# A hybrid attention and RWKV-7 layer on one core: key norms and values by transposes with sums on VectorE, and a new order of the planned region

## The chip, the cores and the metric

The kernel runs on one core of a Trainium2 chip. The metric is the device time of one execution in microseconds (us). The engines are TensorE (PE, with its weight loads as PEld), VectorE (DVE), ScalarE (ACT), GpSimd (POOL) and SyncE (SP, which here issues most transfers). Each works through its own queue in order and waits on semaphores for the others. SBUF is the on-chip memory; PSUM is the accumulator memory that TensorE writes, eight buffers of 128 x 512 floats here.

## The reference

One decoder layer over 16 meta tokens and 512 tokens of width 1024, all in float32. A layer norm feeds one wide projection (w_in), whose columns serve sliding-window attention (16 query heads, 2 key/value heads, window 128, a sink per head, relative bias), an RWKV-7 time mix with 16 heads of 64, and two gates. The two branches are merged by sigmoid gates, projected (w_out), normed, passed through a squared-ReLU MLP of width 4096, and normed again. What the change touches is in the time mix:

```python
kk = kh * k_k
kk = kk / jnp.maximum(jnp.sqrt(jnp.sum(kk * kk, -1, keepdims=True)), 1e-12)   # key norms, per head and token
def step(S, inp):                                   # S: 64 x 64 per head
    sa = jnp.einsum('bhij,bhj->bhi', S, -kk_t)
    S = S * w_t[..., None, :] + sa[..., None] * (kk_t * a_t)[..., None, :] + v_t[..., None] * k_t[..., None, :]
    return S, jnp.einsum('bhij,bhj->bhi', S, r_t)
ym = jnp.mean(y, -1, keepdims=True)                 # per head and token
yv = jnp.mean(jnp.square(y - ym), -1, keepdims=True)
y = ((y - ym) * lax.rsqrt(yv + GN_EPS)) * lnx_g + lnx_b
```

## The kernel before

**Stages.** After the first layer norm (function `lead`), the activations lie transposed in SBUF as hhi and hlo, a high and a low part in the reduced format float32r. A weight block of 128 columns comes by DMA as wraw, is split by ACT (whi, L611) and DVE (wlo, L613), and three float32r products per slice (`three`, L454 to L456) add up to float32 precision. `dense` runs one such block; `shifted` adds the token shift at the eviction (ACT L653, DVE L656). Work that is not of this kind, the attention scores and the whole time mix, uses plain fp32 products or transposes against the constant ident.

**The time mix.** The 16 heads go in eight pairs, j = 0 to 7, each on 128 partitions (64 per head). `rwkv(j)` issues, for one pair: the projections k, r, v; sq, the squared scaled keys; `norms` (L984), which sums sq over the 64 rows of a head for each token by products with the constant ones2; from it d1, its maximum with 1e-24 and its reciprocal (L992, L994), spread by POOL into dv and dvx (L999, L1008). Eight chunks of 64 tokens then get score products (L1031), whose lower triangle NT is inverted: blocks go by DMA to DRAM and back as Nf, POOL does a substitution of 31 steps (L1122, L1126), the blocks come back by DMA as XB, and DVE transposes parts into U (L1153). Two small products (`inv3` L1146, `inv4` L1151) join the blocks. `fold_w` (L1166) and `fold_g` (L1182) fold the inverse into G, whose last additions are DVE L1186. `turn_v` (L1093) brings the values v to token order, and with the constant center (identity minus the mean over a head) removes the mean over the head's 64 values, so that the outputs come out with a mean of zero. `meta0` (L1193) does it for the meta tokens, whose own small chain is L1205, L1209, L1213. The chain over the chunks is seven `link` products (L1243), each followed by `follow`, which writes the new state Z (DVE L1225 for one head, ACT L1228 for the other). `outs` (L1253) gives Y in PSUM. Then the group norm: squares on ACT (L1264), their sum on DVE (L1265), scale and epsilon (L1266), the power -0.5 on POOL (L1267), the multiplication (L1268), and `turn_y` (L1273). The last pair does this in two halves of 256 columns, since nothing comes after it but the w_out products (`project_out`, L1418 to L1420) and the first norm of `first_norm` (L1482 to L1514).

**What sets the order.** All of this, from `lead` to the first up-projections, is a list of operations in a plan. Each operation names its engine, what it reads and writes, and a cost; each buffer belongs to a ring of a few tiles (rg is the ring of the eight PSUM buffers, named g in the trace). The table ORDER gives the sequence in which all operations are issued, hence the order on every engine, and SLOTS says which tile of its ring each buffer takes. The costs given to `op` are not used when the kernel is built. Behind the region comes the feed-forward part, which has an order written by due times of its own.

## Time and profile before

| what | value |
|---|---|
| median of 3 runs | 897.04 us (896.89 to 897.99) |
| profiled execution | 897.01 us, span 895.2 us, granted TensorE clock 0.994 |
| busy, TensorE / VectorE / ScalarE / GpSimd | 874.7 / 674.4 / 518.8 / 263.2 us |
| HBM traffic | 107.56 MB read, 8.21 MB written |

The span runs from the first to the last instruction on the core. Rows of the timeline read: start in us, duration in us, engine, line, operation, out<-in by the program's names, partitions and size, and the number of instructions that the row holds; in brackets the time that the engine was idle before it, and what ended that. A row of windows reads: stretch, its length, then busy time and number of instructions of TensorE, its weight loads, VectorE, ScalarE and GpSimd, the granted clock of TensorE, the busy share of the DMA engines and GB/s. Rows of one line's instructions give minimum, median and maximum in ns. Matmuls are pipelined, so a row's duration overlaps the next; the time that a product costs is the distance between starts.

### The profile page before, as it was taken

The numbers are of one execution on the slowest core, as the hardware profiler recorded it, in microseconds if no ns is written. First come the engines' busy times: TensorE is split into PE (matmuls) and PEld (weight loads), VectorE is DVE, ScalarE is ACT, GpSimd is POOL, SyncE is SP. The second block draws the span as 40 slices with busy tenths as digits, with TensorE's granted clock in tenths as the row PEclk, the third lists the DMA queues.
The fourth block names the chain that finished last, engine by engine and source line by source line (L and its number), as shares of the span: only waits on it lengthen the run. The fifth ranks groups of instructions, "written<-read, shape, count | busy, mean of one in ns | idle before, by whom it ended". The sixth has DMA issues, their size and how long they took to land.

```text
span 895.2 us, 17524 instructions
## 1 busy us (share of the span) xinstructions
PE 874.7 (98%) x6712; PEld 768.1 (86%) x6712; DVE 674.4 (75%) x1192; ACT 518.8 (58%) x1131; POOL 263.2 (29%) x672
## 2 busy tenths in 40 slices
PE   7999999999999999999989999999999999999996
PEld 6999989888898998887878877988898989888885
DVE  6882976868868678478497689598877896788757
ACT  7854568466575494483663745765556655564710
POOL 3138164183461721822816502000010000000001
PEclk9999999999999999999989999999999999999999
DMA  7443323424143242223243631395687578576322
GB/s 272 127 130 104 86 75 107 117 64 131 55 123 101 78 109 85 84 70 101 72 109 102 197 102 59 97 299 132 178 209 216 141 202 256 133 209 165 98 91 94
DMA packets 73533, 115.87 MB, mean 129 GB/s; under 512 B 40311, under 2 KB 47737, under 8 KB 69481
## 3 DMA queue, kind: packets, MB, share of 16 engines
q1 hardware_dynamic: 69728, 98.89, 35.5%
q0 software_dynamic: 2880, 14.68, 9.0%
q8 instruction: 53, 0.87, 0.4%
q10 hardware_dynamic: 840, 1.17, 0.4%
q14 instruction: 32, 0.25, 0.1%
HBM read 107.56 MB, written 8.21 MB: 129 GB/s over the span
## 4 chain that ended last, share of the span: by engine, by line
PE 90%; DVE 8%; issue 1%; ACT 1%; DMA 1%; POOL 0%; DVEq 0%; SPq 0%; ACTq 0%
PE g L454 12%; PE g L455 11%; PE g L456 11%; PE dnR L1798 7%; PE rq L1704 5%; PE tp L1704 4%; PE dnP L1798 4%; PE last L1798 4%; PE dnT L1798 3%; PE up L454 3%; PE up L455 3%; PE up L456 3%; PE g L1243 2%; PE g L1182 2%; PE g L1297 2%; PE g L1031 1%
## 5 line engine op out<-in xcount | busy, mean ns | idle before, releaser
L454 PE MATMUL g<-hhi,whi 128*128 128x512 f32 (+3 forms) x640 | 213.1, 333 | 0.2 <-DVE GR L1045 0.2
L455 PE MATMUL g<-hlo,whi 128*128 128x512 f32 (+3 forms) x640 | 204.0, 319 | 1.6 <-DVE hlo L817 1.6
L456 PE MATMUL g<-hhi,wlo 128*128 128x512 f32 (+3 forms) x640 | 203.6, 318 | 0.0
L454 PEld LDWEIGHTS g<-hhi,whi 128*128 128x128 f32 x640 | 121.0, 189 | 12.6 <-issue 2.2
L455 PEld LDWEIGHTS g<-hlo,whi 128*128 128x128 f32 x640 | 121.2, 189 | 9.6 <-DVE hlo L817 2.1
L456 PEld LDWEIGHTS g<-hhi,wlo 128*128 128x128 f32 x640 | 120.9, 189 | 8.5 <-DVE wlo L613 0.2
L613 DVE TENSOR_TENSOR wlo<-wraw,whi 128x512 fp32r<-128x512 f32 x126 | 88.3, 708 | 30.4 <-ACT whi L611 29.9
L1122 POOL TENSOR_TENSOR ftmp<-Xf,Nf 108x84 f32<-108x84 f32 (+23 forms) x248 | 86.8, 350 | 74.9 <-DMA Nf<-Nd 45.9
L611 ACT CAST whi<-wraw 128x512 fp32r<-128x512 f32 x126 | 77.0, 619 | 54.0 <-PE g L455 24.6
L1126 POOL TENSOR_TENSOR Xf<-Xf,ftmp 108x84 f32<-108x84 f32 (+23 forms) x248 | 89.6, 361 | 19.0
L1788 POOL DMA_DIRECT2D braw<-in_w_ff_dram x12 | 10.7, 890 | 206.1 <-DVE wlo L1605 87.2
L1228 ACT ACTIVATE Z<-g,PC 64x64 f32<-64x64 f32 x64 | 19.7, 308 | 65.2 <-DVE Z L1225 39.9
L1267 POOL TENSOR_TENSOR rs<-rs,mhalf 128x8 f32<-128x8 f32 (+1 forms) x9 | 14.9, 1659 | 76.2 <-DVE rs L1266 76.2
L1605 DVE TENSOR_TENSOR wlo<-wraw,whi 128x1024 fp32r<-128x1024 f32 x22 | 26.9, 1222 | 13.2 <-ACT whi L1601 10.6
L1225 DVE TENSOR_SCALAR Z<-g,PC 64x64 f32<-64x64 f32 x64 | 17.6, 274 | 23.3 <-PE g L1243 20.8
L1601 ACT CAST whi<-wraw 128x1024 fp32r<-128x1024 f32 x22 | 22.9, 1042 | 17.5 <-PE dnR L1798 8.7
L1605 DVE TENSOR_TENSOR wlo<-braw,whi 128x1024 fp32r<-128x1024 f32 x25 | 30.5, 1219 | 2.4 <-ACT whi L1601 2.4
L1605 DVE TENSOR_TENSOR blo<-braw,bhi 128x1024 fp32r<-128x1024 f32 x25 | 30.5, 1219 | 1.6 <-ACT bhi L1601 1.5
L1601 ACT CAST whi<-braw 128x1024 fp32r<-128x1024 f32 x25 | 26.3, 1053 | 5.4 <-PE rq L1704 4.6
L656 DVE SCALAR_TENSOR_TENSOR res<-g,vc,res 128x256 f32<-128x256 f32 (+2 forms) x34 | 16.2, 481 | 17.0 <-ACT res L653 16.8
L1601 ACT CAST bhi<-braw 128x1024 fp32r<-128x1024 f32 x25 | 26.3, 1051 | 3.4 <-DMA braw<-in_w_ff_dram 3.4
L454 PE MATMUL up<-h1hi,whi 128*128 128x512 f32 x72 | 28.1, 390 | 0.0
(532 smaller groups left out, 2469.6 us busy)
## 6 DMA issues: line engine op xcount, KB each, us to landing
wraw<-in_w_in_dram SPq DMA_DIRECT2D x52, 512.0 KB
braw<-in_w_ff_dram SPq DMA_DIRECT2D x19, 1024.0 KB
wraw<-in_w_ff_dram SPq DMA_DIRECT2D x32, 512.0 KB
braw<-in_w_ff_dram POOLq DMA_DIRECT2D x12, 1024.0 KB, 8.8
wraw<-in_w_out_dram SPq DMA_DIRECT2D x14, 256.0 KB
Nf<-Nd SPq DMA_DIRECT2D x24, 144.0 KB
res<-in_x_dram SPq DMA_DIRECT2D x4, 512.0 KB
G<-in_consts_dram SPq DMA_DIRECT2D x16, 128.0 KB
```

Of the source, the lines that this page charges most:

```text
L454: pe.matmul(ps, whi, xhi, start=first, stop=False)
L455: pe.matmul(ps, whi, xlo, start=False, stop=False)
L456: pe.matmul(ps, wlo, xhi, start=False, stop=last)
L611: AC(512, lambda hi=hi, qs=qs: act.copy(hi.t, raw.t[:, qs]), plain=True, r=[raw], w=[hi], new=[hi])
L613: f = lambda hi=hi, lo=lo, qs=qs, e=e: e.tensor_tensor(lo.t, raw.t[:, qs], hi.t.bitcast(F32), op=ALU.subtract)
L1122: sub(nj * nt, lambda s=s, nj=nj, nt=nt, tv=tv: pool.tensor_tensor(tv(), Xf.t[:, 0:nj, s : s + 1].to_broadcast([NB, nj, nt]), Nf.t[:, s : ...
L1126: sub(nj * nt, lambda s=s, nj=nj, tv=tv: pool.tensor_tensor(Xf.t[:, 0:nj, s + 1 :], Xf.t[:, 0:nj, s + 1 :], tv(), op=ALU.add), port=1, r=[ ...
L1228: op("ACT", 335, lambda: act.activation(Z.t[H2[1], c, 1, :], src(1), AF.Copy, scale=PC.t[H2[1], last : last + 1]), r=[ps, PC], w=[(Z, ("s" ...
L1601: act.copy(like(s["r"][0][:, :n], s["x"]), s["x"])
L1605: dve.tensor_tensor(lo, s["x"], hi.bitcast(F32), op=ALU.subtract)
L1704: pe.matmul(o, l[:, ks], r[:, k], start=start and k == c == 0, stop=stop and k == 3 and c == 2, skip_group_check=True)
L1798: pe.matmul(acc[b], l[:, as_], r[:, ws], start=first and i == 0 and q == 0, stop=last and i == NP - 1 and q == 2, skip_group_check=True)
```

## The change

The products with ones2 in `norms` become transposes of sq into a PSUM buffer of their own, kt_ (the first 128 tokens' into mt), and VectorE sums 64 columns at a time. The products with center in `turn_v` and `meta0` become transposes, so that the values keep their mean; the outputs are centred instead: VectorE sums each head's 64 outputs (ym) and subtracts the mean on the way from PSUM to SBUF (yn), and the squares and the last multiplication read yn. The constants center and ones2 go, and with them 130 columns of the constants' transfer. ORDER and SLOTS are new throughout, the opening included.

```diff
 ORDER = [
-    0, 1, 26, 2, 3, 127, 5, 128, 4, 67, 30, 29, 27, 131, 68, 6, 34, 69, 7, 36, 8, 28, 42, 243,
+    0, 6, 2, 7, 26, 8, 41, 42, 67, 3, 68, 5, 69, 9, 43, 47, 70, 44, 60, 10, 48, 49, 71, 11,
...
     bones = (p[:, None] // HD) == (p[None, :] // HD)
-    out["center"] = np.eye(P) - bones / HD
-    out["ones2"] = (p[:, None] // HD) == np.arange(2)[None, :]
...
+    rym = ring("ym", rb, [P, 8], 2)
...
-        mt, d1, dv, dvm = Buf(rg), Buf(rd1), new("dv", rdv), Buf(rdvm)
+        mt, kt_, d1, dv, dvm = Buf(rg), Buf(rg), Buf(rd1), new("dv", rdv), Buf(rdvm)

         def norms():
             for i in range(4):
                 t0 = NMETA + i * P
-                pe.matmul(mt.t[:, 2 * i : 2 * i + 2], sq.t[:, t0 : t0 + P], cv("ones2"), start=True, stop=True)
-            pe.matmul(mt.t[:, 8:10], sq.t[:, 0:P], cv("ones2"), start=True, stop=True)
+                pe.transpose(kt_.t[:, i * P : (i + 1) * P], sq.t[:, t0 : t0 + P], ident)
+            pe.transpose(mt.t[:, P : 2 * P], sq.t[:, 0:P], ident)
             pe.matmul(mt.t[0:48, 32:64], BKm.t, AXm.t.rearrange("p e t -> p (e t)"), start=True, stop=True)

-        op("PE", 1300, norms, r=[sq, BKm, AXm], w=[(mt, "s")], new=[mt], mode="F")
-        op("DVE", 80, lambda: dve.tensor_scalar(d1.t, mt.t[:, 0:10], 1e-24, None, op0=ALU.max), r=[(mt, "s")], w=[d1], new=[d1])
-
-        op("DVE", 120, lambda: dve.reciprocal(d1.t, d1.t), r=[d1], w=[d1])
+        op("PE", 760, norms, r=[sq, BKm, AXm], w=[(mt, "s"), kt_], new=[mt, kt_], mode="F")
+        DV(512, lambda: dve.tensor_reduce(d1.t[:, 0:8], kt_.t.rearrange("p (u i) -> p u i", i=HD), axis=AX.X, op=ALU.add), r=[kt_], w=[d1], new=[d1])
+
+        def inverse():
+            dve.tensor_reduce(d1.t[:, 8:10], mt.t[:, P : 2 * P].rearrange("p (u i) -> p u i", i=HD), axis=AX.X, op=ALU.add)
+            dve.tensor_scalar(d1.t, d1.t, 1e-24, None, op0=ALU.max)
+            dve.reciprocal(d1.t, d1.t)
+
+        op("DVE", 400, inverse, r=[(mt, "s"), d1], w=[d1])
...
         def turn_v():
             for i in range(4):
                 t0 = NMETA + i * P
-                pe.matmul(vt.t[:, i * P : (i + 1) * P], v.t[:, t0 : t0 + P], cv("center"), start=True, stop=True)
+                pe.transpose(vt.t[:, i * P : (i + 1) * P], v.t[:, t0 : t0 + P], ident)
...
         def meta0():
             pe.transpose(ms.t[0:48, 320:448], BKm.t, ident)
-            pe.matmul(ms.t[:, 0:P], v.t[:, 0:P], cv("center"), start=True, stop=True)
+            pe.transpose(ms.t[:, 0:P], v.t[:, 0:P], ident)
...
-            AC(n, lambda cs=cs: act.activation(ysq.t[:, cs], Y.t[:, cs], AF.Square), r=[(Y, k) for k in yk(j, h)], w=[(ysq, h)], new=[ysq] if one else [])
+            DV(n, lambda us=us, u8=u8: dve.tensor_reduce(ym.t[:, us], u8(Y.t), axis=AX.X, op=ALU.add), r=[(Y, k) for k in yk(j, h)], w=[(ym, h)], new=[ym] if one else [])
+            DV(n, lambda us=us, u8=u8: dve.scalar_tensor_tensor(u8(yn.t), B64(ym.t[:, us], HD), -1.0 / HD, u8(Y.t), op0=ALU.mult, op1=ALU.add),
+               r=[(ym, h)] + [(Y, k) for k in yk(j, h)], w=[(yn, h)], new=[yn] if one else [])
+            AC(n, lambda cs=cs: act.activation(ysq.t[:, cs], yn.t[:, cs], AF.Square), r=[(yn, h)], w=[(ysq, h)], new=[ysq] if one else [])
...
-            DV(n, lambda us=us, u8=u8: dve.tensor_tensor(u8(yn.t), u8(Y.t), B64(rs.t[:, us], HD), op=ALU.mult),
-               r=[(rs, h)] + [(Y, k) for k in yk(j, h)], w=[(yn, h)], new=[yn] if one else [])
+            DV(n, lambda us=us, u8=u8: dve.tensor_tensor(u8(yn.t), u8(yn.t), B64(rs.t[:, us], HD), op=ALU.mult),
+               port=1, r=[(rs, h)], w=[(yn, h)])
```

In the changed file the lines of `three` are 453 to 455, and the time mix stands five to eight lines lower: `link` is L1248, `outs` L1258, `inv3` L1151, `inv4` L1156.

The order of the instructions moves in the whole region. The first of the places that matter here is on TensorE, at the chain of links of pair 5. Before, the pair's value transposition (L1096) and weight products (L454 to L456) stand between some of the links (L1243); L1366 are attention outputs and L1031 the scores of the next pair:

```order
L1366 MATMUL g<-pall_194,vtok_216 64x128 x2
L1366 MATMUL g<-pown_195,vdif_218 64x128 x2
L1031 MATMUL g<-G_143,BK_140 128x128 x8
L1243 MATMUL g<-Z_180,G_144 128x128
L1096 MATMUL g<-con,res_127 128x128 x4
L1243 MATMUL g<-Z_180,G_144 128x128 x3
L454 MATMUL g<-hhi,whi 128x512
L455 MATMUL g<-hlo,whi 128x512
L456 MATMUL g<-hhi,wlo 128x512
```

Now (L1187 is `fold_g`, L1036 the scores, L1248 `link`, L1258 `outs`):

```order
L1187 MATMUL g<-GR_165,AT_178 128x128 x16
L1036 MATMUL g<-G_143,BK_140 128x128 x8
L1248 MATMUL g<-Z_179,G_144 128x128 x7
L1258 MATMUL g<-Z_179,G_144 64x64 x16
L1374 MATMUL g<-pall_196,vtok_218 64x128 x2
L1374 MATMUL g<-pown_197,vdif_220 64x128 x2
```

All seven links now stand in a row, and the attention outputs have moved from before the links to behind the outputs. Before, six weight products each stand ahead of the fifth and the sixth link, and the last two links are adjacent.

The second place is on TensorE too, at the inverse of pair 6 (`inv3` is L1146 before, L1151 now; `inv4` L1151 and L1156; L1205, L1209, L1213 are the meta tokens' chain, L1297 attention scores). Before:

```order
L1031 MATMUL g<-G_144,BK_140 128x128 x8
L1205 MATMUL g<-SVm_166,AKm_168 16x64 x2
L1297 MATMUL g<-khi_214,e_133 128x256 x4
L1209 MATMUL g<-RHm_174,XTm_176 16x64 x2
L1146 MATMUL g<-U_185,NT_162 32x32 x16
L1213 MATMUL g<-SVm_166,BTm_172 64x64 x2
L1151 MATMUL g<-XB_181,U_185 32x32 x16
L454 MATMUL g<-hhi,whi 128x266
```

Now (between L1214, the former L1209, and this piece stand twelve more products of L453 to L455, L1218 and three more):

```order
L453 MATMUL g<-hhi,whi 128x266
L454 MATMUL g<-hlo,whi 128x266
L455 MATMUL g<-hhi,wlo 128x266
L1151 MATMUL g<-U_185,NT_162 32x32 x16
L453 MATMUL g<-sghi,gwh_202 128x512
L454 MATMUL g<-sglo,gwh_202 128x512
L455 MATMUL g<-sghi,gwl_204 128x512
L1156 MATMUL g<-XB_181,U_185 32x32 x16
```

Weight products have moved ahead of `inv3`, 18 in all, and the three of a gate (sghi, sglo) between `inv3` and `inv4`.

The third place is on VectorE, at the second half of the last pair's group norm. Before (L1265 to L1268 are the norm, L1387 and L1388 the merge with the attention, L1412 its low part, L613 weight halves, L1482 and L1484 the residual addition and its statistics):

```order
L1387 TENSOR_TENSOR z_207<-z_207,e_130 128x256
L1388 TENSOR_TENSOR z_207<-z_207,e_132 128x256
L613 TENSOR_TENSOR wlo<-wraw,whi 128x512
L1412 SCALAR_TENSOR_TENSOR hlo<-z_207,hhi 128x256
L1265 TENSOR_REDUCE rs_189<-e_135 128x4
L1266 TENSOR_SCALAR rs_189<-rs_189 128x4
L613 TENSOR_TENSOR wlo<-wraw,whi 128x512
L1482 SCALAR_TENSOR_TENSOR res_129<-res_129,g 128x512
L1484 BN_STATS fst_6271<-res_129 128x6
L1482 SCALAR_TENSOR_TENSOR res_126<-res_126,g 128x512
L1268 TENSOR_TENSOR e_133<-g,rs_189 128x256
```

Now (L1269 and L1270 are the mean's sum and the centring, L1273 to L1276 the former L1265 to L1268, L1490 the former L1482):

```order
L1269 TENSOR_REDUCE ym_190<-g 128x4
L1270 SCALAR_TENSOR_TENSOR e_133<-ym_190,g 128x256
L1395 TENSOR_TENSOR z_209<-z_209,e_130 128x256
L1396 TENSOR_TENSOR z_209<-z_209,e_132 128x256
L1273 TENSOR_REDUCE rs_189<-e_135 128x4
L1274 TENSOR_SCALAR rs_189<-rs_189 128x4
L1420 SCALAR_TENSOR_TENSOR hlo<-z_209,hhi 128x256
L613 TENSOR_TENSOR wlo<-wraw,whi 128x512
L1276 TENSOR_TENSOR e_133<-e_133,rs_189 128x256
L1490 SCALAR_TENSOR_TENSOR res_126<-res_126,g 128x512
```

The mean and the centring have come in ahead of the merge, and the multiplication (L1276) stands ahead of the residual additions instead of behind two of them.

More of the change, by code (lines that the diff above doesn't have):

```diff
@@ L1095, in turn_v @@
                 t0 = NMETA + i * P
-                pe.matmul(vt.t[:, i * P : (i + 1) * P], v.t[:, t0 : t0 + P], cv("center"), start=True, stop=True)
-        op("PE", 896, turn_v, r=[v], w=[vt], new=[vt, Z], mode="F")
+                pe.transpose(vt.t[:, i * P : (i + 1) * P], v.t[:, t0 : t0 + P], ident)
+        op("PE", 442, turn_v, r=[v], w=[vt], new=[vt, Z], mode="T")
         for q in range(2):
@@ L1194, in meta0 @@
             pe.transpose(ms.t[0:48, 320:448], BKm.t, ident)
-            pe.matmul(ms.t[:, 0:P], v.t[:, 0:P], cv("center"), start=True, stop=True)
-        op("PE", 335, meta0, r=[BKm, v, XTm, AKm], w=[(ms, 0), (ms, "b")], new=[ms, BTm, SVm, RHm], mode="F")
+            pe.transpose(ms.t[:, 0:P], v.t[:, 0:P], ident)
+        op("PE", 225, meta0, r=[BKm, v, XTm, AKm], w=[(ms, 0), (ms, "b")], new=[ms, BTm, SVm, RHm], mode="F")
         DV(128, lambda: dve.tensor_tensor(BTm.t, ms.t[0:48, 320:448].rearrange("p (h j) -> p h j", h=2), B64(dvm.t, HD), op=ALU.mult),
@@ L1257, in rwkv @@
                w=[(Y, h)], new=[Y] if h == 0 else [], mode="C")
-        ysq, yn, rs = Buf(re_), Buf(re_), Buf(rrs)
+        ysq, yn, rs, ym = Buf(re_), Buf(re_), Buf(rrs), Buf(rym)
         yt, z = Buf(rg), new("z", rz)
```

321 rows, old and new, of tables (ORDER, SLOTS) are left out of this document.

## The prediction

> **What bounds the kernel now.** I read the page first: span, busy shares, slices and clock. Then the windows, to see where TensorE has slack, and TensorE's timeline at the places that the change touches.
>
> ```profile
> span 895.2 us, 17524 instructions
> PE 874.7 (98%) x6712; PEld 768.1 (86%) x6712; DVE 674.4 (75%) x1192; ACT 518.8 (58%) x1131; POOL 263.2 (29%) x672
> PEclk9999999999999999999989999999999999999999
> ```
>
> ```profile
> 0.00:24.00 24.00, 17.73 (x123) 16.19 (x124) 17.23 (x38) 18.55 (x38) 10.01 (x25) 1.00 0.73 254
> 24.00:590.00 566.00, 559.29 (x4966) 492.26 (x4965) 419.58 (x863) 342.35 (x872) 231.41 (x624) 0.99 0.37 103
> 590.00:895.00 305.00, 297.68 (x1628) 259.61 (x1626) 237.60 (x292) 157.91 (x223) 21.79 (x24) 0.99 0.60 169
> ```
>
> TensorE (PE) is the bound: 559.3 us busy of the 566 between 24 and 590 us, where the planned region lies. What leaves its stream shortens the kernel as long as its small waits stay small. VectorE (DVE) has 419.6 of the same 566 us: room, though at single places it already decides. The feed-forward part after 590 us keeps its code, and I cost it at nothing.
>
> The profiled execution took 897.01 us, 1.8 more than its span, and the median of the runs is 897.04; so the sum is made against 897.0.
>
> **The change, part by part.** *1. Fewer passes on TensorE.* The rows show that a plain fp32 product of 128 columns is two matmul records and a transpose is one.
>
> ```profile
> 44.81 0.95 PE L987 MATMUL g<-con,res 128*128 128x2 f32 x8
> 45.62 0.36 PE L988 MATMUL g<-con,res 128*128 128x2 f32 x2
> 45.91 0.27 PE L989 MATMUL g<-AXm,BKm 128*48 128x32 f32 x2
> 104.30 1.05 PE L1096 MATMUL g<-con,e 128*128 128x128 f32 x8
> 105.11 0.37 PE L454 MATMUL g<-hhi,whi 128*128 128x264 f32 x1
> 552.33 0.60 PE L1500 MATMUL g<-con,res 128*128 128x128 f32 x4
> 552.69 0.48 PE L1418 MATMUL g<-whi,hhi 128*128 128x512 f32 x1
> 553.00 0.39 PE L1419 MATMUL g<-wlo,hhi 128*128 128x512 f32 x1
> 553.23 0.40 PE L1420 MATMUL g<-whi,hlo 128*128 128x512 f32 x1
> ```
>
> The four centring products of turn_v are 8 records, and the next instruction starts 0.81 us after the first; four transposes at L1500 are 4 records and take 0.36. So four records less are worth 0.45 us, 0.11 each. The norms are 10 records over 1.10 us (44.81 to 45.91), the same 0.11 although they yield only two columns each. Per pair five records go in norms, four in turn_v and one in meta0: 10 x 0.11 x 8 pairs = **-8.8 us**. The lower bound is the mean pitch, 0.81/8 = 0.10, or -8.1; the upper is 0.1125, or -9.0. I take 0.11, since the marginal record is what goes.
>
> *2. Fewer returns to the long products.* The first wide product after a burst starts its follower 0.31 us later (552.69 to 553.00), the next 0.23: a return costs 0.08. Counted over the two orders, TensorE comes back from small work to weight products 136 times before and 131 times after: **-0.4 us**.
>
> *3. Pair 6's inverse gets its cover back.* In the stretch where the triangular inverse of pair 6 is put together, TensorE stands before both of its steps, and then the clock halves.
>
> ```profile
> 462.15 0.39 PE L1209 MATMUL g<-RHm,XTm 16*16 16x64 f32 x4
> 463.72 0.24 PE L1146 MATMUL g<-U,NT 32*32 32x32 f32 x2 [1.18 <-DVE U L1153]
> 464.19 1.06 PE L1146 MATMUL g<-U,NT 32*32 32x32 f32 x30 [0.22 <-DVE U L1153]
> 466.08 1.06 PE L1151 MATMUL g<-XB,U 32*32 32x32 f32 x32 [0.42 <-ACT U L1155]
> 467.29 0.56 PE L454 MATMUL g<-hhi,whi 128*128 128x266 f32 x1 [0.15 <-DVE GR L1045]
> 470.44 1.35 PE L1166 MATMUL g<-AT,XB 64*64 64x128 f32 x32
> 474.71 0.39 PE L454 MATMUL g<-hhi,whi 128*128 128x266 f32 x1
> 476.31 0.28 PE L454 MATMUL g<-hhi,whi 128*128 128x264 f32 x1
> ```
>
> ```profile
> 464.00:465.00 1.00, 0.81 (x29) 0.81 (x30) 0.97 (x4) 0.00 (x0) 0.00 (x0) 0.58 0.45 66
> 470.00:471.00 1.00, 1.00 (x15) 0.76 (x17) 1.00 (x3) 0.00 (x0) 0.00 (x0) 0.50 0.11 41
> ```
>
> The waits are 1.18 + 0.22 + 0.42 = 1.8 us. The new order puts 18 projection products and the gate's three ahead of or between these steps (second excerpt of the order), some 2.9 us, so I take all of it: **-1.8**. The bounds are -1.8 and nothing, the latter if the transfers behind U come later by as much. The granted clock is 0.58 in 464-465 and 0.50 still in 470-471. Twelve products from 467.29 to 470.44 take 3.15 us, the twelve of the same width from 474.71 to 476.31 take 1.60. That is 1.55 us lost there; with half of the whole stretch of some 6.7 us as the other end (3.4), I take **-2.0** for a stretch that keeps its clock, near the lower end, as half of that time was spent waiting anyway.
>
> *4. Pair 5's state chain loses its cover.* Each link (L1243) needs the state that ACT and DVE write after the one before. Where two links stand next to each other, TensorE waits:
>
> ```profile
> 410.37 0.49 PE L1243 MATMUL g<-Z,G 128*128 128x128 f32 x2 [0.71 <-ACT Z L1228]
> 411.57 0.49 PE L1243 MATMUL g<-Z,G 128*128 128x128 f32 x2 [0.71 <-ACT Z L1228]
> 416.06 0.49 PE L1243 MATMUL g<-Z,G 128*128 128x128 f32 x2 [0.79 <-ACT Z L1228]
> 407.98 0.49 PE L1243 MATMUL g<-Z,G 128*128 128x128 f32 x2
> ```
>
> ```profile
> 405.14 2.47 DVE L1186 TENSOR_TENSOR G<-G,g 128x512 f32<-128x512 f32 x4
> ```
>
> Before, three of the six gaps are bare; after, all six (first excerpt): 3 more x 0.74 = +2.2 us. Also the eight attention products no longer stand between the fold and the first link. The fold's additions on DVE end at 407.61, 0.4 us before the first link started; taking away some 1.0 us of cover shows about +0.7. Together **+2.9**. The bounds are +2.2 and +3.6 (if the first link waits for all it lost).
>
> These seven links at 1.2 us each are over 8 us in which TensorE works less than half the time. The window before shows three such links at full clock:
>
> ```profile
> 410.00:412.00 2.00, 0.91 (x5) 0.72 (x6) 0.85 (x2) 1.23 (x3) 0.00 (x0) 1.00 0.44 64
> ```
>
> The stretch in point 3 shows the other outcome after a similar thinning. I take an even chance of a half-clock stretch of 2.0 us: **+1.0**; ends nothing and 3.4.
>
> The Trainium skill ("TensorE: Matmul & The Clock Gate", section "What's actually happening") has the clock fall after an idle window of about 3.4 us. Here it fell after a wait of 1.18 us amid thin work, so the measurement differs from the plain reading of that rule. By the rule alone the gaps of 0.7 us would never halve the clock, and the sum would be 1.0 us lower.
>
> *5. VectorE's new work.*
>
> ```profile
> L1265 DVE TENSOR_REDUCE rs<-e x6: 420/686/686, 145.7 to 544.0; 128x8 f32<-128x512 f32 x4, 128x4 f32<-128x256 f32 x2
> L1268 DVE TENSOR_TENSOR res<-g,rs x6: 677/682/693, 149.2 to 492.4; 128x512 f32<-128x512 f32 x6
> ```
>
> Per pair come a reduction of 512 columns for the norms (0.69), one of 128 (between nothing and the 0.42 of 256 columns; 0.25, by its size), the mean's reduction (0.69) and the centring (0.68, the nearest row with one PSUM operand): 2.3 us, 18.5 in all. DVE goes from 419.6 to 438 us of some 558, 74 to 79%. The maximum and the reciprocal stay; the last multiplication only changes its source. Ahead of the norms' 1/x it puts 0.9 us into the chain that leads by way of POOL's spreading to NT; NT also waits for the score products, which stand behind the norms in all pairs, and the substitution on POOL follows. That cover hides it in most pairs; if it goes, a pair loses up to 0.9 us at its inverse. kt_ takes one more of the eight PSUM buffers until its reduction has run. For what queues behind the 18.5 us on DVE (weight halves, evictions of the projections) I take **+1.0**: ends nothing and the rival below.
>
> *6. The last pair's output chain.* Its two halves are normalised with nothing but w_out products to hide behind.
>
> ```profile
> 535.95 0.69 PE L1253 MATMUL g<-Z,G 128*64 128x64 f32 x16
> 540.41 0.38 PE L1273 MATMUL g<-con,e 128*128 128x128 f32 x2
> 542.39 0.69 PE L1253 MATMUL g<-Z,G 128*64 128x64 f32 x16
> 547.95 0.38 PE L1273 MATMUL g<-con,e 128*128 128x128 f32 x2
> ```
>
> ```profile
> 543.60 0.38 ACT L1264 ACTIVATE e<-g 128x256 f32<-128x256 f32 x1
> ```
>
> ```profile
> 544.73 1.55 POOL L1267 TENSOR_TENSOR rs<-rs,mhalf 128x4 f32<-128x4 f32 x1 [2.52 <-DVE rs L1266]
> ```
>
> ```profile
> 547.35 0.42 DVE L1268 TENSOR_TENSOR e<-g,rs 128x256 f32<-128x256 f32 x1
> ```
>
> The chain gains a reduction and a centring, 0.42 each, 0.9 with the hand-overs. In the second half 21 w_out products stand between, as before (4.8 us). The new chain is 0.42 + 0.42 + 0.38 + 0.42 + 1.55 + 0.42 plus the small addition and the hand-overs, some 4.4. It fits, because the multiplication, which began 1.1 us after POOL's power had ended, now stands ahead of the residual additions (third excerpt). In the first half the cover shrinks from 4.46 us to twelve products and three links, 12 x 0.23 + 3 x 0.3 = 3.7; the chain of about 4.4 sticks out by 0.7 at most, by nothing if DVE is free at once. I take **+0.5**. The transposes standing there also hold back the second half's outputs behind them.
>
> The opening's order is new too. TensorE is idle 6.3 of its first 24 us, waiting for x and its norm; I take no change, with 1 us either way.
>
> Sum: -8.8 - 0.4 - 1.8 - 2.0 + 2.9 + 1.0 + 1.0 + 0.5 = -7.6: **889.4 us**.
>
> **The rivals.** *Everything hides.* The half-clock stretch goes, the links keep their clock, DVE and the last chain cost nothing: 897.0 - 8.8 - 0.4 - 1.8 - 2.0 + 2.2 = 886.2, and 884.5 to 887 with the bounds. For it: DVE is idle a fifth of the region. Against: six bare links stand in the order.
>
> *DVE comes onto the path.* In a pair where its additions are not hidden, TensorE loses up to the 2.3 us of that pair. One or two such pairs beyond the sum give 892 to 894.5; three or four give it all back, 896 to 898.5. For it: DVE already ends several of TensorE's waits in the rows above. Against: 566 us hold only 6.7 us of PE idle in all.
>
> *The clock falls in more pairs: slower.* Forty norm, 32 value and eight meta products become transposes, in stretches that are thin already. If each pair's stretch of small work now ends like the one of pair 6, each costs 2.0 us and its wait. The gain of 7.6 is gone with the fourth additional stretch; five to eight give 899 to 905. For it: the one stretch quoted. Against: 410-412 was as thin and ran at 1.00. The Trainium skill (same page, section "Part 4: PE-mode transpose") says that transposes do not count as activity for the clock gate in the same way. No row here separates this; by that rule this rival is the outcome.
>
> *The change does not do what it says* (a transpose taking two passes too) is excluded by L1500: four transposes, four records, 0.36 us.
>
> **How the numbers follow.** The sum's case, 887 to 892, has 0.52; everything hides, 0.16; DVE on the path in one or two pairs, 0.21, in three or four, 0.06; the clock, 0.05. 0.2% of 897 is 1.8 us, about what a measurement here can tell from no change. Faster by more is 0.52 + 0.16 + 0.21 = 0.89, within it 0.06, slower 0.05. The range takes the sum's case, 0.13 of the case below it and 0.15 of the 0.21 above: 884.5 to 894.0.
>
> **What would show it.** In the trace of after: one record per norm, value and meta transpose and some 80 records fewer; no wait before inv3 of pair 6 and a clock of 1.00 there; six waits of some 0.7 us in a row at pair 5's links; DVE at about 692 us; waits by DVE at the last pair's transposes. The prediction is wrong if TensorE's idle time between 24 us and the region's end grows from 6.7 to over 12 us, or if the clock is at half in more than two stretches.

## The result, and the profile after

The changed kernel takes 905.62 us in the median (904.77 to 907.78, four runs) against 896.96 us (896.15 to 897.99): ratio 1.010 [1.0079, 1.0120]; the brackets are a 95% interval. It is 8.7 us slower where 7.6 us less had been forecast, 11.6 us above the range. The profiled execution took 906.05 us, its span is 904.3.

The page of after, for the three lines shown of before:

```profile
span 904.3 us, 17360 instructions
PE 874.5 (97%) x6632; PEld 758.1 (84%) x6632; DVE 691.9 (77%) x1226; ACT 518.9 (57%) x1131; POOL 277.3 (31%) x672
PEclk9999999999999999998999989999999999999999
```

TensorE has 80 matmul records fewer, as forecast, and is busy for just as long (874.5 us against 874.7). VectorE is at the forecast 692. GpSimd, whose instructions did not change, is busy 14 us longer. The windows tell where TensorE stands. First two stretches of after, then one of before:

```profile
0.00:24.00 24.00, 16.11 (x112) 14.74 (x112) 16.04 (x36) 17.46 (x36) 9.59 (x31) 1.00 0.66 221
24.00:600.00 576.00, 561.68 (x4898) 484.55 (x4899) 438.91 (x900) 345.35 (x876) 245.85 (x617) 0.99 0.36 104
```

```profile
24.00:600.00 576.00, 569.29 (x5010) 500.55 (x5009) 428.59 (x873) 349.57 (x881) 232.49 (x625) 0.99 0.38 107
```

TensorE's idle time between 24 and 600 us grew from 6.7 to 14.3 us, beyond the 12 that the prediction named as the sign of its failure. Another 1.6 us were lost before 24 us. The two come to 9.2 us, about the 8.7 by which the kernel is slower. TensorE's busy time should have fallen with the 80 records, by the forecast some 9 us, and it did not, since stretches in which little streams count as busy as well: short products in a row, and half clock. How much each of these takes was not separated.

What the prediction said of single places stands in the timeline of TensorE. A pair's norms now take 0.63 us from their first row to the product behind them (459.54 to 460.17), where 1.10 stood before; the inverse of pair 6 has no wait ahead of its two steps (470.04 and 471.77); pair 5's links have their waits:

```profile
459.54 0.60 PE L987 MATMUL g<-con,res 128*128 128x128 f32 x4
459.97 0.27 PE L988 MATMUL g<-con,res 128*128 128x128 f32 x1
460.17 0.23 PE L989 MATMUL g<-AXm,BKm 128*48 128x32 f32 x1
...
470.04 0.91 PE L1151 MATMUL g<-U,NT 32*32 32x32 f32 x32
...
471.77 0.69 PE L1156 MATMUL g<-XB,U 32*32 32x32 f32 x32
```

```profile
408.28 0.49 PE L1248 MATMUL g<-Z,G 128*128 128x128 f32 x2
409.48 0.49 PE L1248 MATMUL g<-Z,G 128*128 128x128 f32 x2 [0.71 <-DVE Z L1230]
...
414.43 0.80 PE L1248 MATMUL g<-Z,G 128*128 128x128 f32 x2 [0.71 <-ACT Z L1233]
415.94 0.80 PE L1248 MATMUL g<-Z,G 128*128 128x128 f32 x2 [0.71 <-DVE Z L1230]
```

The windows of after show the granted clock: half behind those links and at the last pair's inverse, full at pair 6's, where it had halved before.

```profile
413.00:420.00 7.00, 5.50 (x54) 4.63 (x54) 4.40 (x10) 1.57 (x5) 0.00 (x0) 0.52 0.63 175
529.00:536.00 7.00, 7.00 (x82) 4.82 (x81) 4.28 (x9) 2.52 (x8) 0.00 (x0) 0.52 0.16 46
```

```profile
464.00:475.00 11.00, 9.66 (x149) 7.71 (x151) 10.65 (x26) 3.67 (x11) 1.26 (x4) 1.00 0.49 123
```

So the places that I had priced came out in kind as forecast, and most of the time went elsewhere. TensorE's waits in after, by line waited for (total, times, longest):

```profile
PE g L688 <- DMA con<-in_consts_dram: 5.4, 1, 5.4
PE g L1248 <- ACT Z L1233: 3.0, 5, 0.7
PE g L1248 <- DVE Z L1230: 1.8, 3, 0.7
PE g L1151 <- DVE U L1158: 1.5, 1, 1.5
...
PE g L1214 <- DVE BTm L1203: 1.1, 2, 0.7
...
PE g L1210 <- DVE BTm L1203: 1.0, 1, 1.0
```

Behind the first row, a transfer of the opening, the link copies (DVE L1230 for one head, ACT L1233 for the other) lead, and the copies of the meta chain are among the next. Neither engine is full (77% and 57%). The reason shows in the timelines of TensorE, VectorE and ScalarE at one such place of after:

```profile
235.04 0.29 PE L1218 MATMUL g<-SVm,BTm 48*64 48x64 f32 x4
```

```profile
237.03 0.27 DVE L1230 TENSOR_SCALAR Z<-g,PC 64x64 f32<-64x64 f32 x1
```

```profile
237.33 0.31 ACT L1233 ACTIVATE Z<-g,PC 64x64 f32<-64x64 f32 x1 [2.63 <-DVE Z L1230]
```

Both copies read the result of L1218, VectorE partitions 0 to 63 and ScalarE 64 to 127. ScalarE has been idle for 2.63 us and the product ended 2 us ago, yet it starts 0.03 us after VectorE's copy. The two readers of one PSUM buffer run one after the other, in the order in which the kernel's text issues them. VectorE comes to its copy late, as it has other work queued ahead, and ScalarE waits for it with all that stands behind. Adding up, over the traces, the time for which an instruction of VectorE or ScalarE waited for nothing but the other engine's earlier access to the buffer, I get 13.6 us in before (46 places) and 29.7 us in after (57). Each such sum moves by up to some 3 us with where the end of a product is put, since the ends are modelled.

### The profile page after: what moved, and what is told of

The parts are those of the page before. It is cut to its first block, busy times and chain, and to the rows that moved or that the text cites. A ratio compares the mean times of both kernels' runs of the same rounds, so it can differ in the third digit from the quotient of the medians.

```text
span 904.3 us, 17360 instructions
## 1 busy us (share of the span) xinstructions
PE 874.5 (97%) x6632; PEld 758.1 (84%) x6632; DVE 691.9 (77%) x1226; ACT 518.9 (57%) x1131; POOL 277.3 (31%) x672
## 4 chain that ended last, share of the span: by engine, by line
PE 80%; DVE 8%; ACT 6%; DMA 3%; issue 1%; SPq 1%; POOL 0%; DVEq 0%; ACTq 0%
PE g L453 10%; PE g L454 9%; PE g L455 9%; PE dnR L1806 7%; PE rq L1712 5%; PE tp L1712 4%; PE dnP L1806 4%; PE last L1806 4%; PE dnT L1806 3%; PE up L453 3%; PE up L455 3%; PE up L454 3%; PE g L1248 2%; PE g L1187 1%; PE g L1305 1%
## 5 line engine op out<-in xcount | busy, mean ns | idle before, releaser
L453 PE MATMUL g<-hhi,whi 128*128 128x264 f32 (+3 forms) x640 | 211.4, 330 | 0.0
L454 PE MATMUL g<-hlo,whi 128*128 128x264 f32 (+3 forms) x640 | 203.4, 318 | 1.1 <-DVE hlo L817 0.8
L455 PE MATMUL g<-hhi,wlo 128*128 128x264 f32 (+3 forms) x640 | 202.9, 317 | 0.0
L453 PEld LDWEIGHTS g<-hhi,whi 128*128 128x128 f32 x640 | 120.5, 188 | 10.5 <-issue 1.9
L454 PEld LDWEIGHTS g<-hlo,whi 128*128 128x128 f32 x640 | 120.6, 188 | 8.7 <-DVE hlo L817 1.1
L455 PEld LDWEIGHTS g<-hhi,wlo 128*128 128x128 f32 x640 | 120.4, 188 | 8.4
L1127 POOL TENSOR_TENSOR ftmp<-Xf,Nf 108x84 f32<-108x84 f32 (+23 forms) x248 | 94.2, 380 | 77.4 <-DMA Nf<-Nd 49.7
L613 DVE TENSOR_TENSOR wlo<-wraw,whi 128x512 fp32r<-128x512 f32 x126 | 87.2, 701 | 28.3 <-ACT whi L611 15.7
L1131 POOL TENSOR_TENSOR Xf<-Xf,ftmp 108x84 f32<-108x84 f32 (+23 forms) x248 | 94.4, 381 | 18.3
L1796 POOL DMA_DIRECT2D braw<-in_w_ff_dram x12 | 10.7, 894 | 202.8 <-DVE wlo L1613 88.1
L1233 ACT ACTIVATE Z<-g,PC 64x64 f32<-64x64 f32 x64 | 19.8, 309 | 63.6 <-PE g L1248 34.2
L1275 POOL TENSOR_TENSOR rs<-rs,mhalf 128x8 f32<-128x8 f32 (+1 forms) x9 | 15.6, 1737 | 91.0 <-DVE rs L1274 88.1
L1230 DVE TENSOR_SCALAR Z<-g,PC 64x64 f32<-64x64 f32 x64 | 17.5, 274 | 31.7 <-ACT Z L1233 21.0
L1248 PE MATMUL g<-Z,G 128*128 128x128 f32 x112 | 25.2, 307 | 5.3 <-ACT Z L1233 3.0
L1248 PEld LDWEIGHTS g<-Z,G 128*128 128x128 f32 x112 | 18.2, 193 | 14.1 <-ACT Z L1233 7.0
L1426 PE MATMUL g<-whi,hhi 128*128 128x512 f32 x64 | 28.0, 438 | 1.0 <-ACT hhi L1419 1.0
```

The lines of the kernel that those rows point to most:

```text
L453: pe.matmul(ps, whi, xhi, start=first, stop=False)
L454: pe.matmul(ps, whi, xlo, start=False, stop=False)
L455: pe.matmul(ps, wlo, xhi, start=False, stop=last)
L613: f = lambda hi=hi, lo=lo, qs=qs, e=e: e.tensor_tensor(lo.t, raw.t[:, qs], hi.t.bitcast(F32), op=ALU.subtract)
L1127: sub(nj * nt, lambda s=s, nj=nj, nt=nt, tv=tv: pool.tensor_tensor(tv(), Xf.t[:, 0:nj, s : s + 1].to_broadcast([NB, nj, nt]), Nf.t[:, s : ...
L1131: sub(nj * nt, lambda s=s, nj=nj, tv=tv: pool.tensor_tensor(Xf.t[:, 0:nj, s + 1 :], Xf.t[:, 0:nj, s + 1 :], tv(), op=ALU.add), port=1, r=[ ...
```

## The experiments

**Which part: the edits or the order?** Four kernels. In the first, the changed code runs in the order of before, each new operation next to the one that it belongs to; in the second, the code of before in the new order. The third and fourth take the norms alone and the values with the centring alone, in the order of before.

```diff
 ORDER = [                                   # changed code, order of before
-    0, 6, 2, 7, 26, 8, 41, 42, 67, 3, 68, 5,
+    0, 1, 26, 2, 3, 127, 5, 128, 4, 67, 30, 29,
...
```

```diff
+                pe.transpose(kt_.t[:, i * P : (i + 1) * P], sq.t[:, t0 : t0 + P], ident)   # norms alone
...
+                pe.transpose(vt.t[:, i * P : (i + 1) * P], v.t[:, t0 : t0 + P], ident)     # values alone
+            DV(n, lambda us=us, u8=u8: dve.tensor_reduce(ym.t[:, us], ...))
```

Changed code, old order:

> The changed code with the order of the kernel before: the same operations in the same sequence, the 18 added VectorE operations (sums and centring of the outputs) put right ahead of the Square that follows them, buffers placed as before where the place is free. Theory O (the loss comes from the new order: its waits at the links of pair 5, ahead of the last pair's inverse and at the tail, with their half-clock stretches): 80 records fewer x 0.11 us = -8.8 are kept, with 1 to 5 us of new waits, so 889 to 893 us, and pair 5's links look as before (three bare gaps). Theory V (the loss comes from the added 18.5 us of VectorE work and the slower GpSimd substitution, whatever the order): 903 to 910 us, since an order made for less VectorE work hides it no better than one made for it.

Measured 920.18 us, ratio 1.0261 [1.0246, 1.0276].

Old code, new order:

> The code before in the changed kernel's order, without the 18 added VectorE operations. Theory O: the waits of the new order stay and the 80 records come back, so 905.6 + 8.8 = 914 us, less what the missing VectorE work gives back, 909 to 915. Theory V: without the added VectorE work the waits go, about 8 us of them, and the records cost 8.8, so 903 to 907; GpSimd's substitution is back at about 350 ns an operation from 380.

Measured 918.17 us, ratio 1.0242 [1.0226, 1.0259].

Norms alone:

> Key norms alone by plain transposes and VectorE sums, in the order before; values, their meta rows and the outputs as before. 40 records fewer x 0.11 us = -4.4. Theory O: 892 to 894 us. Theory V: the 512-wide sum stands ahead of the inverse's work on VectorE in each of eight pairs, about 0.6 us each, and the substitution slows, so 896 to 900.

Measured 905.04 us, ratio 1.0096 [1.0079, 1.0113].

Values alone:

> Values and their meta rows alone by plain transposes, outputs centred on VectorE, in the order before; key norms by products as before. 40 records fewer x 0.11 us = -4.4. Theory O: 892 to 895 us. Theory V: the centring delays the outputs' chain by about 1.3 us a part and takes a VectorE port from GpSimd, so 899 to 905, most of it in the last pair, whose output chain has the least cover.

Measured 910.58 us, ratio 1.0153 [1.0133, 1.0174].

(A ratio is always to the kernel before, timed in the same round.) All four lie above both expectations: either half alone makes the kernel before slower, and so does the order alone. Read across, the edits gain 12.6 us in the new order (918.17 to 905.62) and cost 23.2 in the old one (896.93 to 920.18). The waits of the norms alone say why the old order does not take them (the lines stand 20 lower than in before):

```profile
PE g L1056 <- DVE e L1046: 2.5, 2, 2.1
...
PE g L1007 <- DVE sb L1328: 1.2, 1, 1.2
...
PE g L1007 <- DVE res L676: 0.9, 1, 0.9
PE g L1007 <- DVE res L1405: 0.9, 1, 0.9
```

L1007 is `norms`, waiting for VectorE to empty the PSUM buffer that kt_ takes; L1056 are the scores. So these kernels tell of edits put where no place had been made for them. The second shows that the new order costs the old code 21.2 us (896.93 to 918.17), where the prediction's terms for the order (2 to 4) add up to -0.3. But this order was made for the changed code, so the old code's longer products stand where no place was made for them either: how much of the 21.2 us the changed code bears is not shown, and the 12.6 us are not what the edits are worth by themselves.

**Two places that the profile showed.** One kernel puts four operations of TensorE that were ready (attention outputs, weight products and the first half of the pair's own outputs) between pair 5's links; one puts the meta tokens' small load ahead of x on SP's queue again, since TensorE's first product waited 5.4 us for the constants, instead of 3.2, though ScalarE's queue sends these at 0.74 us in both.

```diff
-    ..., 2061, 2075, 2271, 2077, 2076, ...
+    ..., 2061, 2075, 2155, 2271, ...         # 2155: attention outputs, 2075: link; likewise 2440, 2441, 2096
```

```diff
-    0, 6, 2, 7, 26, 8,                       # 26: meta tokens, 2: x
+    0, 6, 26, 2, 7, 8,                       # (the first two transfers of SP exchanged)
```

Links covered:

> The changed kernel with four TensorE operations, which were ready by then, moved up between the links of pair 5: 0.93, 0.97, 0.97 and 0.49 us of products in four of the six bare gaps (they stood right behind the links). Theory O (the order left the links bare, and the thin stretch halves the clock): 3.4 us of waiting are filled, and the half clock of 413.3 to 420.1 us, which costs up to 3.4 us of work, goes or shrinks to one of its two 3.41 us windows: 899 to 902.5 us. Rival (the time of the stretch is set by what comes behind it, VectorE's and ScalarE's work for the next products): the gap opens again behind the links and the time stays at 904 to 906.

Measured 905.78 us, ratio 1.0106 [1.0093, 1.0119], as the change itself. The gaps left the links and one came back right behind them, at the weight product that needs the buffer VectorE empties (the timeline of TensorE; lines 21 lower):

```profile
420.19 0.79 PE L474 MATMUL g<-hhi,whi 128*128 128x512 f32 x1 [2.26 <-DVE G L1067]
420.78 0.63 PE L475 MATMUL g<-hlo,whi 128*128 128x512 f32 x1
421.21 0.63 PE L476 MATMUL g<-hhi,wlo 128*128 128x512 f32 x1
```

The 0.43 us from one start to the next behind it, instead of 0.23, are half clock again. VectorE's queue set the pace of that place, not the cover of the links.

Meta first:

> The changed kernel with the first two transfers of SP's queue exchanged: the small load of the meta rows ahead of the first block of x, as in the kernel before. Theory O: the identity lands at 3.2 us instead of 5.4 and the first product starts 2.2 us earlier, of which 1 to 2.2 reach the end: 903.4 to 904.6 us. Rival (the block of x lands later and the first normalization with it): 905 to 906.

Measured 903.82 us (901.59 to 908.38), ratio 1.0096 [1.0077, 1.0115]. The first product starts at 3.26 us. The median is 1.8 us below after, but the runs spread over 6.8 us, so by itself this is no more than a sign.

**Orders searched anew, without the buffer's rule.** For both codes I took an order from a search over durations and hand-overs read from the traces, in which each access to a PSUM buffer waited only for what it needed.

```diff
-    0, 6, 2, 7, 26, 8, 41, 42, 67, 3, 68, 5,      # changed code
+    2, 26, 0, 6, 4, 42, 7, 3, 8, 30, 131, 9,
...
-    0, 1, 26, 2, 3, 127, 5, 128, 4, 67, 30, 29,   # code of before
+    0, 2, 6, 3, 1, 26, 127, 5, 7, 8, 9, 4,
```

Changed code:

> The changed code with its operations put in another order: from the changed kernel's order, operations were moved one at a time within their dependences wherever the durations and latencies read from the traces of these six kernels, with the substitution on GpSimd and the transfers taken at their longer values, said that TensorE ends earlier; places of the buffers unchanged. Theory O (the edits are worth 8 us and the order lost them): 880 to 893 us, with one half-clock stretch at most. Theory V (the added VectorE work and the slower GpSimd cost it in any order): 897 to 905.

Measured 924.40 us, ratio 1.0316 [1.0298, 1.0334].

Code of before:

> The code before with its operations put in another order in the same way and with as many moves, from the order before. Theory O: 8 us above the changed code so reordered, for its 80 records x 0.11 us; 888 to 900 us. Theory V: no slower than the changed code so reordered, at 885 to 895, since it has 18.5 us less VectorE work.

Measured 940.04 us, ratio 1.0484 [1.0466, 1.0502].

Both miss the first range expected by 30 to 50 us. A reckoning without the rule can pick orders that the rule then punishes: 34.1 and 31.7 us of waits for the other engine's access, where before has 13.6. It is not the whole miss, as the weight products' durations had been averaged over their widths too. Setting the reckoned starts beside the real ones led to the places where a start lies 0.03 us behind the other engine's end, as at 237.33 above.

**The rule by itself.** To test it alone, two kernels keep every instruction and the sequence of every engine. Only the interleaving of the engines in the text is changed, and with it which of two engines comes first on a PSUM buffer. In the changed kernel 34 such pairs are exchanged so that the one that can go early is first (27 are link copies, four L1366 with L1367, three on the meta chain); in the kernel before 41 pairs are exchanged the wrong way.

```diff
-    1190, 1088, 1104, 1530, 1340, 1105, 1281, 1341,      # changed; 1104: DVE L1230, 1105: ACT L1233, at 237 us
+    1341, 1089, 1105, 1492, 1568, 1182, 1190, 1530, 1342, 1088, 1343, 1104, 1281, 1090,
...
-    2758, 2380, 2570, 2542, 2381, 2580, 2382, 2362, 2589, 2588, 2377, 2577,   # before; 2380: ACT L1216, 2377: DVE L1198
+    2588, 2377, 2380, 2577,
```

Changed kernel, better interleaving:

> The changed kernel with the same instructions in the same order on every engine; only the text of the program interleaves the engines' work otherwise, so that in 34 pairs of operations of two engines on one PSUM bank the other one stands first (27 of them VectorE's and ScalarE's copies of a link). Theory B (work of two engines on one PSUM bank runs in the order of the text, and in the new order the second one too often waits for a first that comes late; in the traces such waits of VectorE and ScalarE sum to 29.7 us in the changed kernel against 13.6 before): 898 to 902 us, and that sum falls below 20. Rival (the queues alone decide; PSUM banks do not tie VectorE to ScalarE): the same queues give the same time, 904 to 907.

Measured 898.47 us (twelve runs), ratio 1.0016 [1.0005, 1.0028]: 7.2 us less than after.

Kernel before, worse interleaving:

> The kernel before with the same instructions in the same order on every engine, and its text interleaved so that in 41 pairs of operations of two engines on one PSUM bank the other one stands first, the wrong one this time. Theory B: the waits of the second readers grow as in the changed kernel, 902 to 908 us. Rival: 896 to 898.

Measured 908.04 us, ratio 1.0123 [1.0105, 1.0141]: 10.7 us more than before.

The first came out in the range that the rule gave, the second at its upper end. The place shown above, now with ScalarE first (timelines of TensorE, ScalarE and VectorE):

```profile
235.39 0.29 PE L1218 MATMUL g<-SVm,BTm 48*64 48x64 f32 x4
```

```profile
235.72 0.31 ACT L1233 ACTIVATE Z<-g,PC 64x64 f32<-64x64 f32 x1 [0.67 <-PE g L1218]
```

```profile
237.37 0.27 DVE L1230 TENSOR_SCALAR Z<-g,PC 64x64 f32<-64x64 f32 x1
```

ScalarE starts as the product ends, 1.65 us before VectorE instead of behind it. TensorE's idle time between 24 and 600 us falls from 14.3 to 9.3 us. In the kernel before with the worse interleaving the same happens the other way round, and TensorE pays for it. Three engines at pair 6's meta chain, then ScalarE at the same place in before:

```profile
468.92 0.39 PE L1205 MATMUL g<-SVm,AKm 16*16 16x64 f32 x4
...
472.25 0.28 PE L1209 MATMUL g<-RHm,XTm 16*16 16x64 f32 x1 [1.87 <-ACT RHm L1216]
```

```profile
471.63 0.28 DVE L1198 TENSOR_TENSOR BTm<-g,dvm 48x128 f32<-48x128 f32 x1
```

```profile
471.94 0.26 ACT L1216 COPY RHm<-g 16x128 f32<-16x128 f32 x1 [4.42 <-DVE BTm L1198]
```

```profile
461.02 0.25 ACT L1216 COPY RHm<-g 16x128 f32<-16x128 f32 x1 [1.47 <-PE g L1205]
```

ScalarE's copy stands 4.42 us for a VectorE instruction whose result it does not use, and TensorE 1.87 us for that copy. In before the copy is first and waits for its product alone. The summed waits of this kind are 19.9 us in the first (after: 29.7) and 32.0 in the second (before: 13.6).

The same choice for the old code in the new order, against its 918.17 (its operations from here on have numbers four lower):

```diff
-    1084, 1100, 1522, 1334, 1101, 1275,                  # 1100: DVE, 1101: ACT, the copies at 237 us
+    1085, 1101, 1184, 1522, 1084, 1523, 1086, 1775, 1100, 1275,
```

> The code before in the changed kernel's order (918.2 us as first run), with the same order on every engine and only the text interleaved otherwise. Theory B: 4 to 8 us less, 910 to 914; the edits are then worth 12 to 15 us in this order (80 records x 0.11 = 8.8, the rest waits). Rival: 917 to 919.

Measured 910.85 us, ratio 1.0165 [1.0147, 1.0183]: 7.3 us less. So the better choice is worth about the same in the new order with either code, with VectorE's new work and without it. The edits gain 12.4 us there (910.85 to 898.47), 12.6 as first interleaved.

**What is left.** Five more kernels go on from there. Two take the first search again, now with the rule, for the changed code and for the old; one adds the early meta load to the better interleaving; one, on top of that, moves operations of TensorE, VectorE and ScalarE among themselves between 396 and 430 us, pair 5's links; one does so there in another way and in two further stretches.

```diff
-    0, 6, 2, 7, 26, 8, 41, 42, 67, 3, 68, 5,      # searched anew: changed code
+    0, 6, 7, 26, 5, 60, 8, 9, 61, 67, 3, 62,
...
-    0, 1, 26, 2, 3, 127, 5, 128, 4, 67, 30, 29,   # and code of before
+    4, 55, 0, 6, 243, 2, 7, 26, 54, 42, 5, 8,
```

```diff
-L1248 MATMUL g<-Z_179,G_144 128x128 x7            # TensorE at pair 5's links: its stretch
-L1258 MATMUL g<-Z_179,G_144 64x64 x16
+L1248 MATMUL g<-Z_179,G_144 128x128
+L1374 MATMUL g<-pall_196,vtok_218 64x128 x2
...
+L1248 MATMUL g<-Z_179,G_144 128x128 x2
+L453 MATMUL g<-hhi,whi 128x512
...
+L1248 MATMUL g<-Z_179,G_144 128x128
+L1258 MATMUL g<-Z_179,G_144 64x64 x8
```

```diff
-L1248 MATMUL g<-Z_179,G_144 128x128 x7            # the same place in the version with three stretches
-L1258 MATMUL g<-Z_179,G_144 64x64 x16
+L1248 MATMUL g<-Z_179,G_144 128x128
+L1036 MATMUL g<-G_143,BK_140 128x128 x8
+L1248 MATMUL g<-Z_179,G_144 128x128
...
+L1248 MATMUL g<-Z_179,G_144 128x128 x3
+L1258 MATMUL g<-Z_179,G_144 64x64 x8
```

Searched anew, changed code and old code:

> The changed code in another order, found by moving operations one at a time with durations from the traces, as the reordered kernels before it, but now with two things that those lacked: work of two engines on one PSUM bank in the order of the text, and the long products' durations by their width. The meta rows are loaded first. Theory B: with those waits known to the search, the 80 records come through, 876 to 890 us. Theory V (the VectorE work added costs it in any order): 895 or more.

Measured 910.17 us, ratio 1.0139 [1.0115, 1.0164].

> The code before, put into another order in the same way and with as many moves. Theory B: 885 to 895 us, 5 to 11 above the changed code so ordered (80 records x 0.11 us = 8.8). Theory V: no slower than the changed code so ordered.

Measured 913.58 us, ratio 1.0184 [1.0163, 1.0205].

Both missed. The changed code is 3.4 us below the old one, each in an order of its own. Of the changed code's first 40 us TensorE worked 29.5, against 33.7 in before, and a step of GpSimd's substitution (L1131) took 430 ns in the mean, against 381 in after: durations taken from one order did not hold in another. How much of the miss that makes is not shown.

Interleaved, meta first:

> The interleaved version of the changed kernel, with the small load of the meta rows first in SP's queue. Theory B with the opening: 898.5 less 1.8 to 2.2, 896 to 897. Rival: the opening is hidden, 898 to 899.

Measured 897.14 us (eleven runs), ratio 0.9995 [0.9985, 1.0006]: 1.3 us below the interleaving alone. The two intervals touch, so the opening's share is small and not sharply measured.

Pair 5's stretch:

> The same, with operations of TensorE, VectorE and ScalarE between 396 and 430 us (pair 5's links and what lies behind them) moved among themselves so that the stretch is not thin. Theory: half a clock over three windows of 3.41 us (407.5 to 417.7 us in the interleaved run) goes, and bare gaps are filled, 3 to 4 us: 892 to 894. Rival (the stretch is bound by ScalarE's and VectorE's chain; filling it moves the gap behind it, as when the links alone were covered): 896 to 897.

Measured 895.40 us (twelve runs), ratio 0.9981 [0.9968, 0.9994]: 1.7 us less than the kernel that it starts from, half of what was expected, and the one version faster than before, by 0.2%. Its runs fall in two groups by granted clock: six at 0.995 to 0.998 took 893.5 to 894.6 us, six at 0.989 to 0.993 took 896.2 to 899.0. So it seems to keep the full clock only in half of its runs. Five pairs of operations on shared buffers changed sides with the move as well, so the gain is not the clock's and the gaps' alone.

Three stretches:

> The same, with the operations of three stretches moved so (396 to 430, 452 to 500 and 512 to 565 us: pair 5's links, pair 6's inverse, the last pair's inverse and links). Theory: 7 us less than the start, 888 to 892 us, at the forecast. Rival: 895 to 898.

Measured 898.79 us, ratio 1.0027 [1.0014, 1.0039]: a miss, and slower than the kernel that it starts from.

Windows of the version with pair 5's stretch (the profiled run is one of the first group) show TensorE's idle time at 8.0 us between 24 and 600 and the full clock over the links; the second fence is the stretch in the version before it, at 0.77:

```profile
24.00:600.00 576.00, 568.04 (x4948) 490.37 (x4948) 450.19 (x912) 352.79 (x884) 246.16 (x618) 1.00 0.38 109
405.00:420.00 15.00, 13.25 (x98) 9.85 (x98) 11.74 (x26) 5.19 (x13) 2.32 (x3) 1.00 0.32 91
```

```profile
405.00:420.00 15.00, 11.45 (x80) 9.13 (x80) 10.78 (x23) 4.82 (x11) 2.67 (x4) 0.77 0.44 121
```

With three stretches moved, half clock stood at 411, 462 and 523 us.

## Why the prediction was wrong

- **Passes (-8.8), right in kind, a little too large.** 80 records fewer; norms, values and the meta values took 17.1 us before and 10.6 in after, 6.5 us less, or 7.4 without a wait of 0.84 us that stands at one of them (464.59). That is 0.09 us a record instead of 0.11, below the lower bound of 0.10. The rival that the change does not do what it says is out. The edits as a whole gained 12.4 to 12.6 us in the new order, with the order held fixed; what of this goes beyond the passes was not separated. The 0.4 us for returns was not tested by itself.
- **Pair 6's inverse (-3.8), confirmed in kind.** No wait ahead of inv3 or inv4, clock 1.00. But 1.6 us of waits stand on the meta chain just ahead of it, at 464.6 and 466.8 us (L1210, L1214), on copies from a buffer that both engines read, nearly the 1.8 us that the term had taken off.
- **Pair 5's links (+3.9), mechanism right, size not settled.** Six gaps of 0.71 us, three more than before, and half clock for 6.8 us behind them; the first link did not wait, as the +0.7 in this term had it. By the trace that is 2.1 us and up to 3.4. Yet removing most of the gaps and the half clock gave 1.7 us, and covering the links alone gave nothing, since VectorE's queue behind them was late as well.
- **The step that failed is the price of the new order.** The sum prices it only at the places that I looked at, -0.3 in terms 2 to 4 and +0.5 in term 6, and puts everything else in the order at nothing without a reason. I compared the sequences engine by engine. Which of two engines comes first on a shared PSUM buffer is in none of these sequences; it is in the interleaving. Choosing that better in 34 pairs of operations took 7.2 us out of the changed kernel, with VectorE's 692 us unchanged. By the kernels' texts the new order turns round 54 such pairs against the old one; 18 of the 34 go back to the side that they had before, and the other 16 are new choices. So 7.2 us is what a better choice is worth in this order, and how much of it the change of order had lost is not shown exactly; a better choice for the kernel before was not tried.
- **VectorE's new work (term 5, +1.0), not shown to cost more.** The old code, which has none of it, lost as much to the interleaving of the new order (7.3 us). In the old order the same work does cost: the norms alone made the kernel 8.1 us slower.
- **The opening (0 with 1 us either way), too low.** One load ahead of another on SP's queue cost 1.3 to 1.8 us by the medians, within the spread of the runs; the first product's start, 5.4 us instead of 3.2, shows it plainly.
- **The last pair's inverse, not foreseen.** TensorE waited 1.5 us there, then ran at half clock (529 to 536 above):

```profile
527.77 0.59 PE L1151 MATMUL g<-U,NT 32*32 32x32 f32 x25 [1.54 <-DVE U L1158]
```

```profile
527.28 0.44 DVE L1158 STREAM_TRANSPOSE U<-XB 32x256 f32<-32x256 f32 x1 [1.35 <-DMA XB<-xtd]
```

  VectorE's transposition waited for a transfer, behind a substitution on GpSimd that ended at 513.2 us instead of 507.8. Between its steps stand a group norm's power (L1275) and a merge (L1285), as they did before, but GpSimd now stood idle 2.87 us ahead of the power, against 1.15, and its last six steps took 0.55 to 0.65 us each, against 0.21 to 0.25:

```profile
501.47 1.65 POOL L1275 TENSOR_TENSOR rs<-rs,mhalf 128x8 f32<-128x8 f32 x1 [2.87 <-DVE sm L1341]
```

  The wait at the last pair's inverse is still there, 1.5 us, in the version with pair 5's stretch.
- **The last output chain (+0.5).** The waits by VectorE that I expected at its transposes did not come; L1281 is not among TensorE's waits. The term had read the new order wrongly: in the first half it has fifteen products and three links ahead of the transposes, not twelve and three, and TensorE takes 5.44 us over them and the outputs ahead of them (543.84 to 549.28), where it took 4.46.
- **The rivals.** VectorE on the path came nearest in kind, since a late VectorE holds others up, but through which engine comes first at shared buffers, and the old code shows it as well. The clock's rival (899 to 905) had the time nearly right and the cause wrong: ahead of the kernel's last microseconds, half clock grew from one stretch of 6.8 us in before to two in after, not five to eight. Transposes as such did not bring it: pair 6's are among them, at 1.00, and the profiled run of the version with pair 5's stretch, which has all of them, shows no half clock before its last 5 us.

Of the 16.2 us between forecast and result, 7.2 were won back by the interleaving, 1.3 by the opening and 1.7 at pair 5's stretch, the last two close to the spread of the runs. The cause of the remaining 6.0 (895.40 against 889.4) stays open. The last pair's inverse is probably a part of it, and so are the passes, which by their own rows come out 1.4 us short of the forecast. GpSimd's substitution steps became longer as well, in means of one step, before and after:

```profile
L1126 POOL TENSOR_TENSOR Xf<-Xf,ftmp 108x84 f32<-108x84 f32 (+23 forms) x248 | 89.6, 361 | 19.0
```

```profile
L1131 POOL TENSOR_TENSOR Xf<-Xf,ftmp 108x84 f32<-108x84 f32 (+23 forms) x248 | 94.4, 381 | 18.3
```

The old code in the new order has GpSimd at 273.0 us (before 263.2, after 277.3), so most of it comes with the order. In the version with pair 5's stretch the step of L1131 still takes 376 ns. What it costs TensorE was not measured by itself.

## What to carry to other kernels

When an order is changed, don't compare it engine by engine only: for every buffer in PSUM that two engines read, see which comes first in the text, and put first the one whose queue is free first. It costs no instruction, and here was worth 7 us of 905 one way and 11 the other. An edit that saves work must be judged in an order made for it, against the old code in an order made for that: the same edits gained 12.5 us in one order and lost 23 in another, and neither is their worth. And a gap that is covered where it shows comes back where the late engine is next needed.

## What the runs showed of the hardware

- **Two readers of a PSUM buffer in turn.** The second reader waits for the first in this program, also where they read disjoint halves of the partitions: ScalarE's copy starts 0.03 us behind VectorE's at 237.33 us in after, and in the interleaved version at 235.72, as the product ends and ahead of VectorE's, where the text has it first. The Trainium skill ("PSUM — Partial Sum Buffer", section "PSUM bank collisions raise a hardware error") has two engines collide on the same bank and the same 32 partitions, reads included, and allows different groups of 32 partitions at once. By that, VectorE's partitions 0 to 63 and ScalarE's 64 to 127 need no order between them. No run here shows it: a version without that wait was not tried.
- **Half clock comes in units of 3.41 us.** In the records of the granted clock the half stretches, but for the one that ends with the kernel, last 3.41 us or a multiple: 6.83 from 464.2 in before, 6.83 from 413.3 and from 529.3 in after, 13.65 from 476.8 with the changed code in the old order. The Trainium skill ("TensorE: Matmul & The Clock Gate", section "What's actually happening") has a free-running window of 3413 ns and a fall after an idle one. The length agrees. The cause does not read as idleness: of the 3.41 us ahead of these four stretches TensorE was busy for 0.60, 0.38, 0.55 and 0.56, with short products and gaps.
